# The product with w_down as seven block products, with weight sums made by adding transfers

## Chip, core, metric

The kernel runs on one core of one Trainium2 chip. The metric is device time in microseconds (us) of one launch. The engines are named as in the profile: PE (TensorE matrix products; PEld is its weight load), DVE (VectorE), ACT (ScalarE), POOL (GpSimd) and SP (SyncE, whose queue issues the transfers of this kernel). Each engine works through its own queue in order; an instruction whose semaphores have not come yet holds up all that stand behind it on that engine.

## What is computed

One decoder block on 1024 tokens of width 1024, in float32: a projection, sparse attention and stick-breaking attention, an output projection, and a gated MLP with a short convolution. The change concerns the last product of the MLP, `w_down`, of shape 2816 x 1024:

```python
u = _rms_norm(h, norm2_w[layer])
up = u @ w_up[layer]
up = lax.conv_general_dilated(up, conv_w[layer], ...) + conv_b[layer]   # causal, width 3
gate, val = up[..., :D_FF], up[..., D_FF:]                              # D_FF = 2816
h = h + (jax.nn.silu(gate) * val) @ w_down[layer]
return _rms_norm(h, final_norm_w)
```

## The kernel before

Each float32 operand is split into a high part of reduced precision (`hi`, made by ACT) and the rest (`lo = raw - hi`, made by DVE or POOL); a product is then three PE instructions, hi·hi, hi·lo and lo·hi, added up in PSUM. `split_w` (L191 to L194) makes the two parts: ACT on L193, the subtraction on L194, on POOL unless another engine is named.

The stages that matter here, in order of time:

- **Stick-breaking attention**, `sb_attend` (about 62 to 345 us). It runs over 48 units; a unit's front (`sb_front`) makes scores on PE (L425, L426, L428), two sigmoids on ACT (L429, L430), a scan on DVE (L436) and then, on POOL, the product `A = A * tt` (L439) and a clearing (L441). Two units later `sb_turn` lets PE transpose that `A` (L455). In between PE does, at a rate set by `PACE`, the projections of the next pair of heads (`sb_project`), whose weights come in halves of 256 KB by SP (L204) into tiles `wr`, and are split by ACT (L193) and POOL (L194) into `wh` and `wl`. These steps are generators; at each `yield` of the attention the caller may let another generator go one step further. The tile framework then fixes one order for each engine.
- **The product with w_up** (`up`, about 835 to 1239 us), already seven block products (P1 to P7) for each of 22 column blocks, with weight sums made on chip. Its result, gated, goes to DRAM as `act_d`, one tile of 128 x 1024 (128 of the 2816 rows, all tokens) for each block; DVE does most of the additions out of PSUM.
- **The product with w_down** (`down`, from 1239 us to the end). For each half `c` of the tokens (4 blocks of 128 rows) eight PSUM banks hold 4 row blocks x 2 column halves. Over the 22 blocks `i` of 128 rows of `w_down`, `load_w` brings a weight tile of 512 KB and splits it on ACT and POOL (`dh`, `dl`), `load_act` brings 256 KB of `act_d` and splits it on ACT and DVE (`ah`, `al`), and each block then has 8 x 3 PE instructions of 512 columns (L1588 to L1590). The first and last GROUP = 4 blocks run bank by bank, so that a bank's sum is ready early. Then the residual is added (L1624, DVE), the row sum of squares is taken (ACT), and the normalised row goes out (`finish`, L1570, L1571, L1574). The first four blocks are fetched during the last block of `up`.

The weights of `down` are read by SP as they are; nothing is done with them earlier in the program, and POOL issues no transfer anywhere.

Of the kernel before, what the change touches and what calls it, by code (L numbers as in the profile page):

```python
# [10 lines left out]
F32 = mybir.dt.float32  # L11
F32R = mybir.dt.float32r
# [68 lines left out]
class Kern:  # L81
# [479 lines left out]
                    nc.vector.memset(self.score[rows, i, cur + 1:16], NEG)  # L561


    def compress_in(self, kv, wp, vp):
# [503 lines left out]
    def run(self):  # L1068
# [15 lines left out]
        with self.pool("sbv", "right") as vp:  # L1084
            st_b, st_a = ExitStack(), ExitStack()
            stk = [None, st_b.enter_context(self.pool("stkb", "right"))]
            stk[0] = st_a.enter_context(self.pool("stka", "right"))
            ops = []
            with self.pool("xin") as xin:
                proj = self.sb_project(0, wp, stk[0], vp, ops, xin)  # L1090
                self.load_norm(xin, vp, mxs, proj, stk[1])
                for _ in proj:
                    pass
            with self.pool("sbw") as work:
                fill, due = iter(()), 0.0
                got = [ops, [], [], []]

                def start(p):
                    nonlocal fill
                    for _ in fill:  # L1100
                        pass
                    if p < 3:
                        fill = self.sb_project(p + 1, wp, stk[1 - p % 2], vp, got[p + 1])
                    else:
                        st_a.close()
                        fill = self.compress_keys(st_a.enter_context(self.pool("cin", "right")), wp, vp)
                    self.pace = PACE[p == 3]
# [7 lines left out]
                for _ in fill:  # L1115
                    pass
            st_a.close()
            st_b.close()
# [148 lines left out]
    def mlp(self, mxs):  # L1267
# [125 lines left out]
        for _ in fill:  # L1393
            pass
        st_r.close()
        self.weights, self.acts = {}, {}
        self.up(p1)
        self.down(st_up)

# [58 lines left out]
    def up(self, p1):  # L1458
# [3 lines left out]
        for i in range(NF):  # L1462
# [45 lines left out]
            u3 = self.scratch()  # L1508
            nc.vector.tensor_add(u3, bc, u2)
            if last:  # L1510
                for j in range(GROUP):
                    if j > 1:
                        self.load_w(j)
                    self.load_act(j, 0)
            bd = self.ps(tags[3])
            self.product(bd, i, "P5", True)

# [14 lines left out]
            gate(1)  # L1532


    def load_w(self, i):

        homes = ((self.qn, 0), (self.qn, 4), (self.mts, 4), (self.mts, 0))
        if i < 2 * len(homes):
            if i in self.weights:
                return  # L1540
            t, lo = homes[i // 2]
            v = t[:, lo:lo + 4].rearrange("p a b t -> p (a b t)")[:, 2048 * (i % 2):2048 * (i % 2) + 2048]
            dh, dl = v[:, 0:T], v[:, T:2048]
        else:
            dh, dl = (self.tl(self.dp, [P, T], t, 5, F32R) for t in ("dh", "dl"))
        raw = self.tl(self.rawp, [P, KT, P], "wr", 4).rearrange("p k c -> p (k c)")
        self.nc.sync.dma_start(raw, self.a["w_down"][i * P:(i + 1) * P, :])
        self.split_w(raw, dh, dl)
        self.weights[i] = (dh, dl)

    def load_act(self, i, c):

        if c == 0 and i < GROUP:
            raw = self.scratch()
            ah, al = (t[:, i, :] for t in self.R["P7"])
        else:
            raw = self.tl(self.dp, [P, 512], "ar", 3)
            ah, al = (self.tl(self.dp, [P, 512], t, 7, F32R) for t in ("ah", "al"))
        self.nc.sync.dma_start(raw, self.act_d[i][:, c * 512:c * 512 + 512])
        self.split_w(raw, ah, al, self.nc.vector)  # L1560
        self.acts[i, c] = (ah, al)

    def down(self, st_up):
        nc, a = self.nc, self.a
        weights, acts = self.weights, self.acts
        rows = []

        def finish(tb, y, ss):
            r = self.rstd(ss, 1, 1.0 / DM, True)
            nc.scalar.activation(y[:, 0:512], y[:, 0:512], AF.Copy, scale=r[:, 0:1])  # L1570
            nc.vector.scalar_tensor_tensor(y[:, 512:DM], hs[tb][:, 512:DM], r[:, 0:1], self.fnw[:, 512:DM],  # L1571
                                           op0=ALU.mult, op1=ALU.mult)
            for i in range(2):
                nc.sync.dma_start(a["out"][tb * P:(tb + 1) * P, i * 512:i * 512 + 512], y[:, i * 512:i * 512 + 512])  # L1574

        hs = {}
        with ExitStack() as st_2:
            for c in range(2):
                banks = {}

                def mms(i, tb, hf):
                    if (tb, hf) not in banks:
                        banks[tb, hf] = self.ps(("o", "z", "z", "z", "mb", "tr", "tr", "ma")[2 * tb + hf])
                    pd = banks[tb, hf]
                    ah, al = acts[i, c]
                    dh, dl = weights[i]
                    s, cs = slice(tb * P, tb * P + P), slice(hf * 512, hf * 512 + 512)
                    nc.tensor.matmul(pd, ah[:, s], dh[:, cs], start=i == 0, stop=False)  # L1588
                    nc.tensor.matmul(pd, ah[:, s], dl[:, cs], start=False, stop=False)  # L1589
                    nc.tensor.matmul(pd, al[:, s], dh[:, cs], start=False, stop=i == NF - 1)  # L1590

                def blocks(first, last, alone):

                    for i in range(first, last):
                        if (i, c) not in acts:
                            self.load_w(i)
                            self.load_act(i, c)
                        if not alone:
                            continue
                        for tb in range(4):  # L1600
                            for hf in range(2):
                                mms(i, tb, hf)

                blocks(0, GROUP, False)
                for tb in range(4):
                    for hf in range(2):
                        for i in range(GROUP):
                            mms(i, tb, hf)
                if c == 0:
                    st_up.close()  # L1610
                    self.dp = self.rawp = st_2.enter_context(self.pool("dp"))
                    self.fnw = self.tl(self.dp, [P, DM], "fnw")
                    nc.sync.dma_start(self.fnw, a["final_norm_w"].rearrange("(o c) -> o c", o=1).to_broadcast([P, DM]))
                blocks(GROUP, NF - GROUP, True)
                blocks(NF - GROUP, NF, False)
                for tb in range(4):
                    row = 4 * c + tb
                    h = hs[row] = self.tl(self.dp, [P, DM], "h", 4)
                    nc.sync.dma_start(h, self.h_d[row])
                    for hf in range(2):  # L1620
                        for i in range(NF - GROUP, NF):
                            mms(i, tb, hf)
                        cs = slice(hf * 512, hf * 512 + 512)
                        nc.vector.tensor_add(h[:, cs], banks[tb, hf], h[:, cs])  # L1624
                    y = self.tl(self.dp, [P, DM], "y", 3)
                    nc.gpsimd.tensor_mul(y[:, 0:512], h[:, 0:512], self.fnw[:, 0:512])
                    ss = self.square_sums(self.tl(self.nt, [P, 512], "na", 2), [h[:, 0:512], h[:, 512:DM]])
                    rows.append((row, y, ss))
                    if len(rows) > 1:
                        finish(*rows.pop(0))  # L1630
            while rows:
                finish(*rows.pop(0))


_INS = ["x", "norm1_w", "w_in", "cmp_pos_k", "cmp_pos_v", "cmp_k_w1", "cmp_k_w2", "cmp_v_w1", "cmp_v_w2",
# [27 lines left out]
```

## Time and profile before

| | us |
|---|---|
| median of 3 runs | 1492.44 |
| lowest and highest | 1489.34, 1494.07 |
| the profiled execution, device time | 1489.68 |
| its span, first to last instruction | 1487.9 |

| engine | busy us | share of the span |
|---|---|---|
| PE | 1432.7 | 96% |
| PEld | 1200.9 | 81% |
| DVE | 979.3 | 66% |
| ACT | 793.7 | 53% |
| POOL | 761.4 | 51% |

The profile is of one execution. Busy time does not count waiting, nor the issuing of transfers. PE's instructions overlap, so its rate is best read from the distance of two starts. A window's row gives, for a stretch of the span, each engine's busy time with the number of its instructions, the granted TensorE clock as a share of full speed, the mean busy share of the 16 DMA engines and the GB/s that they moved.

### The profile page before, as it was taken

The page shows a single profiled execution, that of the slowest core. Times are in us where ns is not written, and L with a number is a line of the kernel's source. Part 1 is how long each engine was busy: PE and PEld are TensorE (multiplying, and loading weights), DVE is VectorE, ACT ScalarE, POOL GpSimd, SP SyncE. Part 2 cuts the span into 40 slices and gives each one's busy share as a digit, 9 for nine tenths or more (in the row PEclk, how much of TensorE's full clock was granted, in tenths as well). Part 3 has the DMA queues.
Part 4 walks back from the last instruction along what each step waited for, and adds up shares of the span by engine and source line. Part 5 has one row for each costly group of instructions (what it writes and reads, how often), then busy time and mean ns, then how long its engine had stood idle before and what let it go on. Part 6 is the DMA issues. An engine that isn't in the chain of part 4 may idle for free. (4 is left out here: it accounts for less than half of the span.)

```text
span 1487.9 us, 21917 instructions
## 1 busy us (share of the span) xinstructions
PE 1432.7 (96%) x7619; PEld 1200.9 (81%) x7619; DVE 979.3 (66%) x2018; ACT 793.7 (53%) x1691; POOL 761.4 (51%) x727
## 2 busy tenths in 40 slices
PE   7999999999899999999998899999999999999998
PEld 5777777777788988998887778888888887888886
DVE  5587878775257899997438687777778775414112
ACT  6576676653368888887324444444444453324122
POOL 3355655562326667664132566666666664545043
PEclk9999999999999999999999999999999999999999
DMA  5200100325311010003340222222222233845321
GB/s 195 71 22 22 29 22 22 96 65 162 113 30 30 1 57 2 1 16 114 128 135 22 78 78 85 86 85 85 85 86 85 79 113 116 298 140 192 103 92 57
DMA packets 113354, 122.75 MB, mean 83 GB/s; under 512 B 6988, under 2 KB 84444, under 8 KB 112988
## 3 DMA queue, kind: packets, MB, share of 16 engines
q1 hardware_dynamic: 113244, 121.36, 25.4%
q8 instruction: 60, 0.98, 0.3%
q14 instruction: 50, 0.41, 0.1%
HBM read 96.58 MB, written 24.75 MB: 82 GB/s over the span
## 5 line engine op out<-in xcount | busy, mean ns | idle before, releaser
L194 POOL TENSOR_TENSOR gl<-mxs,gh 128x512 fp32r<-128x512 f32 x88 | 116.5, 1325 | 66.3 <-ACT gh L193 63.0
L439 POOL TENSOR_TENSOR A<-A,tt 128x384 f32<-128x384 f32 (+3 forms) x96 | 95.8, 1002 | 97.1 <-DVE tt L436 50.5
L194 POOL TENSOR_TENSOR gl<-wr,gh 128x512 fp32r<-128x512 f32 x66 | 85.7, 1301 | 103.2 <-ACT gh L193 80.5
L194 DVE TENSOR_TENSOR al<-ar,ah 128x512 fp32r<-128x512 f32 x40 | 42.1, 1063 | 128.6 <-ACT ah L193 110.4
L194 POOL TENSOR_TENSOR dl<-wr,dh 128x1024 fp32r<-128x1024 f32 x28 | 69.7, 2495 | 102.8 <-ACT dh L193 90.7
L186 DVE TENSOR_TENSOR pl<-ps_tr,ph 128x512 fp32r<-128x512 f32 (+1 forms) x175 | 111.9, 642 | 13.1 <-ACT ph L185 11.6
L185 ACT ACTIVATE ph<-ps_tr 128x512 fp32r<-128x512 f32 (+1 forms) x175 | 98.0, 563 | 42.0 <-PE ps_tr L455 24.8
L193 ACT ACTIVATE gh<-mxs 128x512 fp32r<-128x512 f32 x88 | 55.3, 629 | 65.3 <-PE ps_ma L1455 22.1
L436 DVE TENSOR_TENSOR_SCAN tt<-tt 128x384 f32<-128x384 f32 (+1 forms) x64 | 69.8, 1093 | 28.3 <-ACT tt L429 27.8
L194 POOL TENSOR_TENSOR wl<-wr,wh 128x512 fp32r<-128x512 f32 x40 | 54.9, 1377 | 62.2 <-ACT wh L193 60.4
L193 ACT ACTIVATE ah<-ar 128x512 fp32r<-128x512 f32 x40 | 25.0, 628 | 110.2 <-PE ps_ma L1589 101.5
L429 ACT ACTIVATE tt<-ps_z 128x384 f32<-128x384 f32 (+3 forms) x96 | 47.6, 496 | 43.0 <-PE ps_z L428 20.2
L734 POOL TENSOR_SCALAR lgw<-lgw,r,gates 128x640 f32<-128x640 f32 (+4 forms) x64 | 48.2, 764 | 36.4 <-DVE r L732 15.7
L193 ACT ACTIVATE gh<-wr 128x512 fp32r<-128x512 f32 x66 | 40.9, 623 | 43.3 <-DMA wr<-w_up_d 15.1
L219 PE MATMUL ps_ma<-uh,wh 128*128 128x512 f32 x136 | 60.4, 444 | 1.2 <-ACT wh L193 1.2
L220 PE MATMUL ps_ma<-ul,wh 128*128 128x512 f32 x136 | 55.2, 406 | 2.1 <-DVE ul L189 2.1
L221 PE MATMUL ps_ma<-uh,wl 128*128 128x512 f32 x136 | 55.2, 406 | 0.6 <-POOL wl L194 0.6
L455 PE MATMUL ps_tr<-ident,A 128*128 128x128 f32 x320 | 49.1, 277 | 6.4 <-DVE pl L186 2.6
L455 PEld LDWEIGHTS ps_tr<-ident,A 128*128 128x128 f32 x320 | 37.1, 142 | 16.0 <-DVE osb L501 3.2
L1483 ACT ACTIVATE na<-na 128x512 f32<-128x512 f32 x44 | 27.6, 628 | 39.9 <-DVE na L1479 39.9
L1434 DVE TENSOR_TENSOR mxs<-mxs,wr 128x512 f32<-128x512 f32 x22 | 35.3, 1604 | 19.8 <-POOL mxs L1433 19.7
L430 ACT ACTIVATE A<-ps_z 128x384 f32<-128x384 f32 (+3 forms) x96 | 47.4, 493 | 0.1
(683 smaller groups left out, 5193.5 us busy)
## 6 DMA issues: line engine op xcount, KB each, us to landing
wr<-w_up_d SPq DMA_DIRECT2D x44, 512.0 KB, 5.0
wr<-w_down_d SPq DMA_DIRECT2D x36, 512.0 KB, 4.7
act_d<-na SPq DMA_DIRECT2D x44, 256.0 KB, 3.9
wr<-w_in_d SPq DMA_DIRECT2D x40, 256.0 KB, 2.8
ar<-act_d SPq DMA_DIRECT2D x40, 256.0 KB, 2.5
h<-h_d SPq DMA_DIRECT2D x8, 512.0 KB, 4.7
out_d<-y SPq DMA_DIRECT2D x16, 256.0 KB, 2.2
mxs<-x_d SPq DMA_DIRECT2D x4, 512.0 KB, 3.5
```

The costliest lines, as they stand in the source:

```text
L185: nc.scalar.activation(hi, src, AF.Copy)
L186: nc.vector.tensor_sub(lo, src, f(hi))
L193: nc.scalar.activation(hi, raw, AF.Copy)
L194: (eng or nc.gpsimd).tensor_sub(lo, raw, f(hi))
L219: nc.tensor.matmul(out, lh, rh, start=(i == 0), stop=False)
L220: nc.tensor.matmul(out, lh, rl, start=False, stop=False)
L221: nc.tensor.matmul(out, ll, rh, start=False, stop=(i == last))
L429: nc.scalar.activation(tt[:, 0:w], z[:, :w], AF.Sigmoid, scale=-1.0)
L436: nc.vector.tensor_tensor_scan(rev, rev, rev, 1.0 if carry[j] is None else carry[j], op0=ALU.mult, op1=ALU.bypass)
L439: nc.gpsimd.tensor_mul(A[:, j, 0:w], A[:, j, 0:w], tt[:, 1:w + 1])
L455: nc.tensor.transpose(pt[:, kk * 256 + j * P:kk * 256 + (j + 1) * P], A[:, j, c0:c0 + P], self.ident)
L734: nc.gpsimd.tensor_scalar(lg[i][:, :L], lg[i][:, :L], r[:, i:i + 1], gate[:, i:i + 1], op0=ALU.mult, op1=ALU.mult)
```

## The change

**In `down`.** The 2816 rows of `w_down` are cut into two halves of 11 blocks, its columns into two halves of 512, and the tokens into two halves of 512. The product of these 2 x 2 blocks is made as seven products in the order P1, P6, P2, P7, P5, P4, P3, each of 11 steps ("units", 77 in all), 4 row blocks and 3 PE instructions of 512 columns. A unit `n` has an operand of activations and one of weights, both 128 x 512. `fetch` issues its transfers by SP, up to 7 units ahead; `halves` forms sums of activations where the product wants one (P6 two subtractions, P7, P5 and P3 one each, all on DVE), and splits both operands on ACT and DVE into one of eight places. Activations that are used again stay in SBUF (`a11`, `a22`, `s2`). PSUM holds four banks for a product; P2 goes on in P1's banks, P4 in P7's, P3 in P5's. `evacuate` adds the banks out, on DVE but for P1; `bring` adds sums to residuals on POOL. POOL no longer splits weights here.

**In `sb_attend`.** Four of the seven products (P5, P7, P6, P4) need sums of weight blocks. A new generator `down_sums` makes them in DRAM, in 4 x 11 tiles `td` of 128 x 512: 44 plain copies DRAM to DRAM issued by SP, and 44 transfers issued by POOL that add a block of `w_down` into the tile. For each of the 11 steps, P5 and P7 are copied from one block and added to once; P6 is copied from P5's sum and added to; P4 from P6's sum and added to. So each step is a chain of six transfers, and each waits for the one before. The generator goes one step at each `yield` of the attention.

```diff
+    def down_sums(self):
+        b = {(i, k): self.a["w_down"].rearrange("(i j p) (k c) -> i k j p c", i=2, p=P, k=2)[i, k] ...}
+        td = self.td = {t: [self.dram.tile([P, 512], F32, name=f"td{t}_{j}") for j in range(n)]
+                        for t in ("P5", "P7", "P6", "P4")}
+        for r in range(n + 5):
+            for lag, dst, src, add in ((0, "P5", b[0, 1], None), (0, "P7", b[0, 1], None), (1, "P5", None, b[0, 0]),
+                                       (1, "P7", None, b[1, 1]), (2, "P6", td["P5"], None), (3, "P6", None, b[1, 1]),
+                                       (4, "P4", td["P6"], None), (5, "P4", None, b[1, 0])):
+                j = r - lag
+                if not 0 <= j < n:
+                    continue
+                if add is None:
+                    nc.sync.dma_start(td[dst][j], src[j])
+                else:
+                    nc.gpsimd.dma_start(td[dst][j], add[j], accum_op=ALU.add)
+                for _ in range(2):
+                    yield
...
+                sums = self.down_sums()
                 for _ in self.sb_attend(start, work, mxs):
+                    next(sums, None)
                     due += self.pace
...
             if last:
                 for _ in range(AHEAD):
                     self.prepare()
-                self.load_w(0)
-                self.load_w(1)
+                for n in range(2):
+                    self.fetch(n)
+                    self.halves(n)
...
-    def load_w(self, i):
-    def load_act(self, i, c):
...
+    DOWN = ("P1", "P6", "P2", "P7", "P5", "P4", "P3")
+    def fetch(self, n):
...
+        if name == "P1":
+            v = act(0, 0, self.scratch() if n < GROUP else keep("a11"))
+        elif name == "P6":
+            v = act(0, 1, passing())
+            act(1, 1, keep("a22"))
+            if j < GROUP:
+                act(0, 0, keep("a11"))
+        elif name in ("P2", "P3"):
+            v = act(1, 0, passing())
+        w = self.scratch()
+        src = {"P1": rows(0)[:, 0:512], "P2": rows(1)[:, 0:512], "P3": rows(1)[:, 512:DM]}
+        nc.sync.dma_start(w, src[name] if name in src else self.td[name][j])
+    def halves(self, n):
...
+        if name == "P6":
+            s2 = kept["s2", j] = self.tl(self.dp, [P, 512], "s2", self.ND)
+            nc.vector.tensor_sub(s2, v, kept["a22", j])
+            nc.vector.tensor_sub(s2, s2, kept["a11", j])
+            v = s2
+        elif name == "P7":
+            v = self.tl(self.dp, [P, 512], "ar", 4)
+            nc.vector.scalar_tensor_tensor(v, kept["s2", j], -1.0, kept["a22", j], op0=ALU.mult, op1=ALU.subtract)
...
+        self.split_w(v, ah, al, nc.vector)
+        self.split_w(w, bh, bl, nc.vector)
...
+        def mms(n, tb):
+            ah, al, bh, bl = self.slots[n]
+            nc.tensor.matmul(bank, ah[:, s], bh, start=first and j == 0, stop=False, skip_group_check=not first)
+            nc.tensor.matmul(bank, ah[:, s], bl, start=False, stop=False, skip_group_check=not first)
+            nc.tensor.matmul(bank, al[:, s], bh, start=False, stop=j == ND - 1, skip_group_check=not first)
```

**The order on the engines.** PE, DVE and ACT have the same instructions in the same order as before up to the last block of `up`. POOL and SP do not.

On POOL, at the start of `sb_attend`. `wl114`, `wl117` and `wl175` are three splits of projection weights, `A101` is the first unit's `A`, and `td...` are the sums. Before:

```order
L194 TENSOR_TENSOR wl114_636<-wr112_634,wh113_635 128x512
L441 MEMSET A101_606 128x128
L194 TENSOR_TENSOR wl117_642<-wr115_640,wh116_641 128x512
L194 TENSOR_TENSOR wl175_919<-wr173_917,wh174_918 128x512
L441 MEMSET A118_646 128x128
L439 TENSOR_TENSOR A101_606<-A101_606,tt102_607 128x128
L439 TENSOR_TENSOR A101_606<-A101_606,tt104_618 128x256
```

After, the end of the same stretch (between `wl114` and these rows stand ten more adding transfers and the clearing of `A101`):

```order
L582 DMA tdP6_4_644<-w_down_d 128x512
L582 DMA tdP4_2_653<-w_down_d 128x512
L582 DMA tdP5_7_625<-w_down_d 128x512
L582 DMA tdP7_7_636<-w_down_d 128x512
L194 TENSOR_TENSOR wl117_687<-wr115_685,wh116_686 128x512
L582 DMA tdP6_5_645<-w_down_d 128x512
L582 DMA tdP4_3_654<-w_down_d 128x512
L582 DMA tdP5_8_626<-w_down_d 128x512
L194 TENSOR_TENSOR wl175_977<-wr173_975,wh174_976 128x512
L441 MEMSET A118_691 128x128
L439 TENSOR_TENSOR A101_606<-A101_606,tt102_607 128x128
L582 DMA tdP7_8_637<-w_down_d 128x512
```

Ten adding transfers stand ahead of `wl114` on POOL, seventeen (14 of them ahead of `wl117`) between it and the first product of `A101`, and the last seventeen between the products of the next five units, the 44th ahead of the product that before started at 89.38 us.

On SP, the same place. `wr115` to `wr234` are halves of projection weights, `bnear_d` and `bcmp_d` tables that go to DRAM. Before:

```order
L533 DMA bnear_d_461<-KA84_470 128x1024
L204 DMA wr115_640<-w_in_d 128x4x128
L536 DMA bcmp_d_462<-KB82_463 128x960
L204 DMA wr173_917<-w_in_d 128x4x128
L204 DMA wr176_923<-w_in_d 128x4x128
L204 DMA wr234_1186<-w_in_d 128x4x128
```

After, from `wr173` on:

```order
L204 DMA wr173_975<-w_in_d 128x4x128
L580 DMA tdP4_0_651<-tdP6_0_640 16x4096
L580 DMA tdP5_5_623<-w_down_d 128x512
L580 DMA tdP7_5_634<-w_down_d 128x512
L580 DMA tdP6_3_643<-tdP5_3_621 16x4096
L580 DMA tdP4_1_652<-tdP6_1_641 16x4096
L580 DMA tdP5_6_624<-w_down_d 128x512
L580 DMA tdP7_6_635<-w_down_d 128x512
L580 DMA tdP6_4_644<-tdP5_4_622 16x4096
```

Ten copies stand ahead of the second `bnear_d` on SP, 18 from there to `wr176`, and 16 behind; each copy out of a `td` tile waits for the adding transfer into it, and the loads of `wr` behind it wait with it.

On DVE, in the last block of `up`, whose additions are L1505, L1509 and L1518 (after: L1533, L1537 and L1545). Before:

```order
L1484 TENSOR_TENSOR na2901_13332<-na2901_13332,nb2888_13254 128x512
L1505 TENSOR_TENSOR mxs_89<-ps_tr2913_13380,mxs_89 128x512
L194 TENSOR_TENSOR P7l2306_9804<-mxs_89,P7h2305_9803 128x512
L1509 TENSOR_TENSOR mxs_89<-ps_tr2914_13394,mxs_89 128x512
L194 TENSOR_TENSOR P7l2306_9804<-mxs_89,P7h2305_9803 128x512 x3
L1518 TENSOR_TENSOR ps_tr2913_13380<-ps_ma2917_13428,mxs_89 128x512
```

After:

```order
L194 TENSOR_TENSOR qn_4037<-mxs_89,qn_4037 128x512 x2
L1511 TENSOR_TENSOR na2901_13464<-na2901_13464,nb2888_13386 128x512
L194 TENSOR_TENSOR qn_4037<-mxs_89,qn_4037 128x512
L1533 TENSOR_TENSOR mxs_89<-ps_tr2911_13516,mxs_89 128x512
L194 TENSOR_TENSOR qn_4037<-mxs_89,qn_4037 128x512
L1537 TENSOR_TENSOR mxs_89<-ps_tr2912_13530,mxs_89 128x512
L194 TENSOR_TENSOR qn_4037<-mxs_89,qn_4037 128x512 x2
L1545 TENSOR_TENSOR ps_tr2911_13516<-ps_ma2913_13556,mxs_89 128x512
```

Where four splits of activations stood among the last additions of `up`, the splits of activations and weights of the first units of `down` stand now, six of them here; more follow among the convolution's instructions.

## Rows read from the trace of the kernel before

**Rows 1.** The page: span, busy times by engine, and the queue's packets, MB, share.

```profile
span 1487.9 us, 21917 instructions
...
PE 1432.7 (96%) x7619; PEld 1200.9 (81%) x7619; DVE 979.3 (66%) x2018; ACT 793.7 (53%) x1691; POOL 761.4 (51%) x727
...
q1 hardware_dynamic: 113244, 121.36, 25.4%
```

**Rows 2.** Windows by stage: attention, `up`, `down` (columns in the first row).

```profile
core 0: us, PE busy (x) PEld busy (x) DVE busy (x) ACT busy (x) POOL busy (x), PEclk, DMA share, GB/s
62.00:345.00 283.00, 271.38 (x1591) 221.18 (x1590) 213.41 (x369) 184.22 (x393) 163.71 (x181) 0.99 0.15 39
835.00:1236.00 401.00, 398.44 (x1757) 328.64 (x1755) 318.32 (x447) 189.58 (x336) 250.59 (x185) 1.00 0.27 85
1239.00:1481.00 242.00, 239.84 (x1057) 197.99 (x1055) 68.99 (x84) 74.59 (x115) 95.42 (x54) 1.00 0.43 150
```

**Rows 3.** Timeline of PE: first and last product of `down` (start, duration).

```profile
1239.00 0.39 PE L1588 MATMUL ps_o<-qn,P7h 128*128 128x512 f32 x1
...
1480.33 0.39 PE L1590 MATMUL ps_ma<-dh,al 128*128 128x512 f32 x1
```

**Rows 4.** Waits of PE from 1215 us on (total, times, longest).

```profile
PE ps_o L1590 <- DVE al L194: 1.9, 1, 1.9
PE ps_ma L1454 <- DVE ps_tr L1518: 0.5, 1, 0.5
```

**Rows 5.** Groups by line from 1270 us (busy, mean ns), and line L194 on DVE (min/median/max).

```profile
L194 POOL TENSOR_TENSOR dl<-wr,dh 128x1024 fp32r<-128x1024 f32 x28 | 69.7, 2495 | 102.8 <-ACT dh L193 90.7 <-DMA h<-h_d 9.0 <-DMA wr<-w_down_d 3.0
L194 DVE TENSOR_TENSOR al<-ar,ah 128x512 fp32r<-128x512 f32 x36 | 35.6, 996 | 115.1 <-ACT ah L193 110.4 <-PE ps_o L1589 4.7
...
L193 ACT ACTIVATE ah<-ar 128x512 fp32r<-128x512 f32 x35 | 21.9, 629 | 106.3 <-PE ps_ma L1589 101.5 <-DMA ar<-act_d 3.2 <-DVE al L194 1.5
...
L194 DVE TENSOR_TENSOR al<-ar,ah x40: 675/694/2896, 1260.8 to 1443.1; 128x512 fp32r<-128x512 f32 x40
```

**Rows 6.** Timeline of POOL at the start of the attention.

```profile
47.55 1.28 POOL L194 TENSOR_TENSOR wl<-wr,wh 128x512 fp32r<-128x512 f32 x1
...
61.14 1.29 POOL L194 TENSOR_TENSOR wl<-wr,wh 128x512 fp32r<-128x512 f32 x1 [12.16 <-ACT wh L193]
...
66.47 1.37 POOL L439 TENSOR_TENSOR A<-A,tt 128x128 f32<-128x128 f32 x2 [1.17 <-DVE tt L432]
...
89.38 1.17 POOL L439 TENSOR_TENSOR A<-A,tt 128x512 f32<-128x512 f32 x1 [1.46 <-PE ps_tr L455]
```

**Rows 7.** Timeline of PE in the same place: transposes of `A` (L455).

```profile
67.96 0.60 PE L455 MATMUL ps_tr<-ident,A 128*128 128x128 f32 x4
...
72.57 0.55 PE L455 MATMUL ps_tr<-ident,A 128*128 128x128 f32 x3 [1.67 <-POOL A L439]
...
93.64 0.60 PE L455 MATMUL ps_tr<-ident,A 128*128 128x128 f32 x4
```

**Rows 8.** Windows around the start of the attention; columns as in rows 2.

```profile
20.00:45.00 25.00, 21.60 (x111) 15.23 (x109) 20.17 (x25) 14.19 (x24) 6.53 (x6) 1.00 0.34 109
45.00:62.00 17.00, 17.00 (x79) 13.90 (x79) 5.50 (x11) 6.16 (x11) 4.19 (x8) 1.00 0.21 62
62.00:80.00 18.00, 15.93 (x90) 12.05 (x88) 13.15 (x25) 13.51 (x31) 11.22 (x14) 1.00 0.13 30
80.00:100.00 20.00, 19.28 (x115) 15.96 (x115) 17.40 (x30) 14.55 (x31) 11.02 (x13) 1.00 0.10 26
100.00:130.00 30.00, 29.19 (x163) 23.24 (x163) 19.61 (x33) 17.93 (x39) 17.07 (x18) 1.00 0.10 26
```

**Rows 9.** Timeline of SP: issues of transfers (start, duration of issuing).

```profile
42.37 0.36 SPq L533 DMA_DIRECT2D bnear_d<-KA  x1
...
1247.88 0.37 SPq L1613 DMA_DIRECT2D fnw<-final_norm_w_d  x1
```

**Rows 10.** The page: issues of transfers, KB each, median us to landing.

```profile
ar<-act_d SPq DMA_DIRECT2D x40, 256.0 KB, 2.5
```

More of the change, by code (lines that the diff above doesn't have):

```diff
@@ L561, in load_tables @@
                     nc.vector.memset(self.score[rows, i, cur + 1:16], NEG)
+    def down_sums(self):
+        nc, n = self.nc, NF // 2
+        b = {(i, k): self.a["w_down"].rearrange("(i j p) (k c) -> i k j p c", i=2, p=P, k=2)[i, k]
+             for i in range(2) for k in range(2)}
+        td = self.td = {t: [self.dram.tile([P, 512], F32, name=f"td{t}_{j}") for j in range(n)]
[13 more added lines that the diff above has]
+                    yield
     def compress_in(self, kv, wp, vp):
@@ L1115, in run @@
                 for _ in fill:
+                    pass
+                for _ in sums:
                     pass
@@ L1395, in mlp @@
         st_r.close()
-        self.weights, self.acts = {}, {}
+        self.raw_ab, self.kept, self.slots = {}, {}, {}
         self.up(p1)
@@ L1510, in up @@
             if last:
[L1511 to L1514, printed above, removed]
+                for n in range(2, GROUP):
+                    self.fetch(n)
+                    self.halves(n)
             bd = self.ps(tags[3])
@@ L1532, in up @@
             gate(1)
-    def load_w(self, i):
[L1537 to L1549, printed above, removed]
@@ L1551, in load_act @@
-    def load_act(self, i, c):
[L1553 to L1561, printed above, removed]
-    def down(self, st_up):
[L1564 to L1576, printed above, removed]
-        with ExitStack() as st_2:
[L1578 to L1604, printed above, removed]
-                for tb in range(4):
[L1606 to L1632, printed above, removed]
@@ new lines, with act, keep, passing @@
+    ND = NF // 2
+    DOWN = ("P1", "P6", "P2", "P7", "P5", "P4", "P3")
+    def fetch(self, n):
+        nc = self.nc
+        name, j = self.DOWN[n // self.ND], n % self.ND
+        def act(b, c, t):
+            nc.sync.dma_start(t, self.act_d[j + b * self.ND][:, c * 512:c * 512 + 512])
+            return t
+        def keep(key):
+            t = self.kept[key, j] = self.tl(self.dp, [P, 512], key, self.ND)
+            return t
+        def passing():
+            return self.tl(self.dp, [P, 512], "ar", 4)
+        v = None
+        if name == "P1":
[8 more added lines that the diff above has]
+        w = self.scratch()
+        rows = lambda b: self.a["w_down"][(j + b * self.ND) * P:(j + b * self.ND + 1) * P, :]
+        src = {"P1": rows(0)[:, 0:512], "P2": rows(1)[:, 0:512], "P3": rows(1)[:, 512:DM]}
+        nc.sync.dma_start(w, src[name] if name in src else self.td[name][j])
+        self.raw_ab[n] = (v, w)
@@ new lines, in halves @@
+    def halves(self, n):
+        nc = self.nc
+        name, j = self.DOWN[n // self.ND], n % self.ND
+        v, w = self.raw_ab.pop(n)
+        kept = self.kept
+        if name == "P6":
[6 more added lines that the diff above has]
+            nc.vector.scalar_tensor_tensor(v, kept["s2", j], -1.0, kept["a22", j], op0=ALU.mult, op1=ALU.subtract)
+        elif name == "P5":
+            v = self.tl(self.dp, [P, 512], "ar", 4)
+            nc.vector.scalar_tensor_tensor(v, kept["s2", j], -1.0, kept["a11", j], op0=ALU.mult, op1=ALU.subtract)
+        elif name == "P4":
+            v = kept["a22", j]
+        elif name == "P3":
+            nc.vector.scalar_tensor_tensor(v, v, -1.0, kept["s2", j], op0=ALU.mult, op1=ALU.subtract)
+        t, lo = ((self.qn, 0), (self.qn, 4), (self.mts, 4), (self.mts, 0))[n % 8 // 2]
+        place = t[:, lo:lo + 4].rearrange("p a b t -> p (a b t)")[:, n % 2 * 2048:n % 2 * 2048 + 2048]
+        ah, al, bh, bl = (place[:, 512 * i:512 * i + 512] for i in range(4))
+        self.split_w(v, ah, al, nc.vector)
+        self.split_w(w, bh, bl, nc.vector)
+        self.slots[n] = (ah, al, bh, bl)
```

96 lines of the change are left out of this document (added).

## The prediction

> **What bounds the kernel now.** I read the busy times of the page first, then windows cut at the stages, then the timelines at the two places that the change touches. PE is busy for 96% of the span [rows 1], and 271.4 of 283 us of the attention, 398.4 of 401 of `up`, and 239.8 of 242 of `down` [rows 2]. Whatever takes instructions from PE shortens the time one for one, and whatever keeps PE waiting lengthens it the same way, because PE has almost nothing to make up with. The transfers are far from full: 0.15 of the DMA engines' time in the attention and 0.43 in `down` [rows 2]. So there are two questions: how much PE work goes from `down`, and whether the sums can be made at the start of the attention without making PE wait. All sums below are made on the profiled execution, 1489.68 us; the median of the three runs is 1492.44, so 2.8 us are added at the end. Differences under 0.3% (about 4.5 us) are about what a measurement of this kernel cannot tell from no change.
>
> **What `down` gains.** Before, PE issues 22 blocks x 8 banks x 3 = 528 instructions for each half of the tokens, 1056 in all. After, 77 units x 4 row blocks x 3 = 924 of the same 512 columns. First product at 1239.00, last at 1480.33 [rows 3], with one stall of 1.9 us on the way [rows 4]: (1480.33 - 1239.00 - 1.9) / 1055 = 0.227 us from start to start. 132 instructions less are 132 x 0.227 = 30.0 us less. The stall of 1.9 us is at the entry, where PE waits for the first splits on DVE; it goes with the code that made it, but the entry is now tighter. Its first group of four units holds 48 instructions (10.9 us) where four blocks held 96 (21.8 us), each needs a weight split on DVE too, and the first loads behind those issued in advance follow the place on SP where the final norm's weight is fetched, at 1247.88 [rows 9]; with 2.5 us to land [rows 10] and two splits, units 4 and up can be late. Between 0 (the loads issued ahead suffice) and 5 us (half of the 10.9) I take 3, nearest to the 1.9 seen at this place. More splits now stand among DVE's last additions of `up`. PE lost 0.5 us to DVE there [rows 4]; between 0 and eight more splits of 0.694 [rows 5], 6 us, I take 1. Together: -30.0 - 1.9 + 3 + 1 = **-27.9 us**, with bounds -32 and -21.
>
> **What could eat that inside `down`.** DVE: 154 splits (both operands of 77 units) and 55 sums (P6 22, P7, P5 and P3 11 each) are 209 operations. The split's median is 0.694 us, its mean from 1270 us on 0.996 [rows 5]. Apart from its 40 splits DVE had 69.0 - 40 x 0.996 = 29 us of work there [rows 2, 5], and has about as much after. At the median that is 209 x 0.694 + 29 = 174 us beside 924 x 0.227 = 210 us of PE; at the mean, 237 us, and DVE would be the bound. I take the median: it is the split's usual time, and what stretches some of them to 2.9 us has as its likeliest partner POOL's 28 splits of 2.5 us in the same window [rows 5], which the change removes. ACT: 154 splits x 0.629 = 97 us [rows 5] and, at most, the 53 us of its other work (74.6 - 35 x 0.629) are 150, under 210. Transfers: 136 operand tiles and 16 of the residual, 0.262 MB each, and 4.2 MB out are 44 MB in 210 us, 210 GB/s. The queue moved 121.36 MB in 25.4% of 1487.9 us [rows 1], that is 321 GB/s when all engines are busy, so a share of 0.65. Covered. The tail behind the last product (1480.7 to 1487.9) keeps its steps; nothing is booked for it.
>
> **What the sums cost.** Their places on the queues decide. Ten adding transfers stand on POOL ahead of the split at 47.55, seventeen between it and the first product of `A` at 66.47, and the other seventeen ahead of the product at 89.38 [rows 6]. On SP ten copies stand ahead of the issue at 42.37 [rows 9], 18 then follow before the last of three weight loads there, and 16 come later. Each is one link of a chain, copy, add, copy, add: POOL's queue stands until a copy has landed, SP's until an add has, and the work queued behind stands with them. On POOL that is the product `A`, and PE reads it at once: its first transposes start at 67.96, 1.5 us after, and the next waited 1.67 us for POOL [rows 7]. So a delay of that product is a delay of PE.
>
> How long do 44 copies and 44 adds take? Free time of the DMA engines, from their share in each window [rows 8]: 25 x 0.66 = 16.5 us from 20 to 45 us, 17 x 0.79 = 13.4 to 62, 18 x 0.87 = 15.7 to 80, 20 x 0.90 = 18.0 to 100, then 0.9 a microsecond. A 256 KB load costs 0.262 MB / 321 GB/s = 0.82 us of all engines. No row shows a transfer from DRAM to DRAM, nor one that adds. Lower bound: each moves as a load does, 0.82. Upper bound: each read and each write is paid for as a transfer of its own, 1.63 for a copy and 2.45 for an add. I take 0.82 for a copy, nearest to the load's row (one read, one write), and 1.63 for an add, as it reads two tiles where a load reads one.
>
> By 45 us: 10 x 0.82 + 10 x 1.63 = 24.5, less 16.5 free, leaves 8.0. Then 18 x 0.82 + 17 x 1.63 = 42.5, so 50.5 before the first `A`. 47.1 us are free by 100 us, and the last 3.4 take 3.8: done at 103.8 and not 66.5, +37.3 us. Then 16 x 0.82 + 17 x 1.63 = 40.8 us, 45.4 at 0.9, where 22.9 us (66.47 to 89.38) stood before: +22.4. Off go 3.1 us between the end of that product at 90.55 and its reader on PE at 93.64 [rows 6, 7], and PE's idle time from 62 to 100 us, 2.1 + 0.7 [rows 8]. The sums cost +37.3 + 22.4 - 5.9 = **+53.8 us**.
>
> The chain's delay alone does not set this: two of 2.5 us [rows 10] per two rounds, 16 rounds, are 40 us, under the 108 us of transfers. POOL's issuing has no row; between SP's 0.36 [rows 9] and a whole operation of POOL, 1.3 [rows 6], 17 of them are 6 to 22 us, inside the time in which it waits for transfers anyway.
>
> The Trainium skill speaks on this point. Its page "Collectives: The Full Stack", section "The bandwidth ceiling: the fold count and why AG ≠ RS ≠ AR", says that a reduction in the DMA path needs two source reads for each write and reaches about half of a copy's rate, 32.35 against 62.28 GB/s. No row here shows such a transfer; by that rule an add is two loads' time and the kernel comes out as I forecast, by the load's row alone it would be 1479 us.
>
> **Sum.** 1489.68 - 27.9 + 53.8 = 1515.6; with 2.8 for the median, **1518 us**.
>
> **Rivals.**
> *The adds run as loads do (faster).* The place is the same, POOL's queue ahead of the first `A`; the price of an add decides. At 0.82 all: 16.4 us by 45, nothing left over; 35 x 0.82 = 28.7 done at 79.5, +13.0; then 33 x 0.82 / 0.9 = 30.1 for 22.9, +7.2; less 5.9 is +14.3. 1489.7 - 27.9 + 14.3 + 2.8 = 1479. For it: the engines pass bytes, and an adder in their way need not cost time. Against: the second read. Between the two ends the cost grows by (53.8 - 14.3) / 0.81 = 48.8 us for each microsecond of an add; it equals the gain at 0.82 + (27.9 - 14.3) / 48.8 = 1.10 us. From there on the kernel is slower. An add between 1.0 and 1.2 us gives no change that can be measured.
>
> *Transfers inside DRAM are dear.* At 1.63 and 2.45: 40.8 - 16.5 = 24.3 left at 45 us; with 71.0 more, 95.3; 47.1 by 100 us and 53.6 after, 153.6, +87.1; then 67.7 / 0.9 = 75.3 for 22.9, +52.4; less 5.9, +133.6. 1598 us. For it: no row bounds the writing into DRAM beside the reading; against: the engines of a load read and write at the same time too.
>
> *`down` does not get what it is meant to.* DVE at 0.996 a time is the bound: 237 us, a gain of 5 and not 28; with the sums at 53.8 that is 1541 us. Against it stand the splits at 0.694 once POOL is away.
>
> **How the numbers follow.** Adds of about 1.2 to 2.3 us, 1498 to 1551 by 48.8 us for each: 0.38, the forecast. Adds as loads: 0.32, faster. An add near 1.1: 0.10, no change. Dear transfers, 1551 and up: 0.15. DVE the bound: 0.05, slower with either price of the adds. So faster 0.32, same 0.10, slower 0.58. The range reaches to the fast rival less the 9 us that the bounds of `down` and a POOL queue with more slack can add, 1470, and into the dear case up to 1580; about 0.06 is left out below and 0.08 above. The forecast's own range is 1498 to 1551.
>
> **What would show it.** After: in the attention's first 80 us, POOL idle ahead of the adds and ahead of the first product of `A`, released by transfers, and PE idle at its first transposes of `A`, some 35 us and then some 20 in pieces; the DMA share near 1 there; the attention later by about 54 us, the rest until `down` unchanged. In `down`, first to last product about 211 to 214 us, PE's waits under 5 us, DVE's splits at 0.69. The forecast is wrong if the share of the DMA engines stays low where POOL waits (then a delay, or the issuing, sets the pace and not the bytes), if PE waits for nothing there, or if `down` takes over 220 us.

## The result and the profile after

The kernel with the change takes 1513.34 us (median of 4 runs, 1512.12 to 1517.48) against 1490.89 us (4 runs). The ratio is 1.0153, with a 95% interval of 1.0125 to 1.018: slower, by 22 us. The profiled execution has a span of 1511.5 us against 1487.9 [rows 1], 23.6 us more.

Page of the changed kernel: span, busy times, DMA queues, the group of POOL's adding transfers, and its issues (KB each, us from issue to landing).

```profile
span 1511.5 us, 22302 instructions
...
PE 1414.0 (94%) x7487; PEld 1185.5 (78%) x7487; DVE 1075.1 (71%) x2191; ACT 821.3 (54%) x1769; POOL 722.4 (48%) x747
...
q1 hardware_dynamic: 126332, 138.14, 28.6%
q0 software_dynamic: 6336, 11.54, 4.7%
...
L582 POOL DMA_DIRECT2D tdP<-w_down_d x44 | 37.8, 891 | 60.9 <-issue 29.4
...
tdP<-w_down_d POOLq DMA_DIRECT2D x44, 256.0 KB, 7.0
```

PE is busy for 18.7 us less, and the span is longer by 23.6. A queue that was not there before, q0, moves the 11.54 MB of the 44 adds in 4.7% of 1511.5 us, which is 71 us of all engines: 1.61 us for each add.

Windows of the changed kernel at the start of the attention, to be held against [rows 8]; the last is `down`.

```profile
core 0: us, PE busy (x) PEld busy (x) DVE busy (x) ACT busy (x) POOL busy (x), PEclk, DMA share, GB/s
20.00:45.00 25.00, 21.62 (x100) 15.58 (x99) 17.91 (x22) 13.10 (x22) 11.84 (x12) 0.86 0.86 218
45.00:62.00 17.00, 17.00 (x81) 13.82 (x80) 8.01 (x12) 6.63 (x12) 9.69 (x13) 1.00 1.07 280
62.00:80.00 18.00, 8.56 (x44) 6.17 (x42) 3.19 (x9) 6.72 (x15) 4.93 (x6) 0.85 1.06 262
80.00:100.00 20.00, 0.48 (x1) 0.18 (x1) 0.84 (x3) 0.85 (x2) 9.63 (x12) 0.50 0.92 182
100.00:130.00 30.00, 22.75 (x110) 18.01 (x110) 17.14 (x27) 14.54 (x30) 18.00 (x23) 0.84 1.01 219
...
1292.80:1502.40 209.60, 209.60 (x925) 173.30 (x923) 163.41 (x248) 100.79 (x189) 34.33 (x31) 1.00 0.56 189
```

From 45 to 130 us the DMA engines are full where before they were busy for 0.10 to 0.21. PE has one instruction from 80 to 100 us. In `down` PE is busy without a gap.

POOL at the same place: the last issues ahead of the first product of `A`, and the 44th add with the product that stood at 89.38 us before [rows 6].

```profile
66.59 0.81 POOL L582 DMA_DIRECT2D tdP<-w_down_d  x1 [5.11 <-DMA tdP<-tdP]
...
96.49 0.83 POOL L582 DMA_DIRECT2D tdP<-w_down_d  x1 [1.34 <-issue]
97.03 1.58 POOL L194 TENSOR_TENSOR wl<-wr,wh 128x512 fp32r<-128x512 f32 x1
...
98.40 0.71 POOL L439 TENSOR_TENSOR A<-A,tt 128x128 f32<-128x128 f32 x1
...
141.51 0.82 POOL L582 DMA_DIRECT2D tdP<-w_down_d  x1 [1.55 <-DVE tt L432]
142.07 1.37 POOL L439 TENSOR_TENSOR A<-A,tt 128x512 f32<-128x512 f32 x1
```

In all, POOL stands for 60.9 us ahead of the adds. The three largest parts of that by what ended them (us, times):

```profile
  issue: 29.4, 20
  DMA tdP<-w_down_d: 13.6, 5
  DMA tdP<-tdP: 7.9, 3
```

So 21.5 us are waits for transfers, as forecast. "issue" is idle time for which the profile names nothing that POOL waited for; what POOL stands for in these 29.4 us is not shown.

What PE waits for from 60 to 400 us (total, times, longest), and the product at which the longest wait ends:

```profile
PE ps_tr L455 <- POOL A L439: 37.1, 4, 28.2
PE ps_tr L455 <- DVE pl L186: 10.9, 8, 6.8
```

```profile
99.17 0.48 PE L455 MATMUL ps_tr<-ident,A 128*128 128x128 f32 x1 [28.23 <-POOL A L439]
```

Forecast were some 35 us in one piece and then some 20 in several.

And PE at both ends of `down`, which answers to [rows 3]:

```profile
1292.81 0.39 PE L1651 MATMUL ps_o<-qn 128*128 128x512 f32 x1
...
1502.02 0.39 PE L1653 MATMUL ps_z<-mts 128*128 128x512 f32 x1
```

So the whole difference lies in three places. `down` starts 53.8 us later (1292.81 against 1239.00), takes 209.2 us from first to last product where it took 241.3, and the tail behind the last product (start of it plus 0.39) is 9.1 us where it was 7.2: 53.8 - 32.1 + 1.9 = 23.6. The last transpose of `A` starts at 393.2 us against 340.4, so 52.8 of the 53.8 us are there at the attention's end.

### The profile page after: what moved, and what is told of

The parts are those of the page before. It is cut to its first block, busy times and chain, and to the rows that moved or that the text cites. A ratio compares the mean times of both kernels' runs of the same rounds, so it can differ in the third digit from the quotient of the medians.

```text
span 1511.5 us, 22302 instructions
## 1 busy us (share of the span) xinstructions
PE 1414.0 (94%) x7487; PEld 1185.5 (78%) x7487; DVE 1075.1 (71%) x2191; ACT 821.3 (54%) x1769; POOL 722.4 (48%) x747
## 3 DMA queue, kind: packets, MB, share of 16 engines
q0 software_dynamic: 6336, 11.54, 4.7%
## 5 line engine op out<-in xcount | busy, mean ns | idle before, releaser
L194 POOL TENSOR_TENSOR gl<-mxs,gh 128x512 fp32r<-128x512 f32 x88 | 116.4, 1323 | 71.8 <-ACT gh L193 68.5
L194 POOL TENSOR_TENSOR gl<-wr,gh 128x512 fp32r<-128x512 f32 x66 | 85.7, 1300 | 103.4 <-ACT gh L193 78.6
L455 PE MATMUL ps_tr<-ident,A 128*128 128x128 f32 x320 | 50.7, 281 | 50.5 <-POOL A L439 37.1
L436 DVE TENSOR_TENSOR_SCAN tt<-tt 128x384 f32<-128x384 f32 (+1 forms) x64 | 69.6, 1089 | 30.3 <-ACT tt L429 28.7
L455 PEld LDWEIGHTS ps_tr<-ident,A 128*128 128x128 f32 x320 | 37.2, 143 | 61.8 <-POOL A L439 47.5
L1687 POOL TENSOR_TENSOR a<-a,p 128x512 f32<-128x512 f32 x8 | 12.5, 1571 | 141.0 <-DVE mts L194 121.5
L194 POOL TENSOR_TENSOR wl<-wr,wh 128x512 fp32r<-128x512 f32 x40 | 56.0, 1404 | 29.1 <-ACT wh L193 27.0
L582 POOL DMA_DIRECT2D tdP<-w_down_d x44 | 37.8, 891 | 60.9 <-issue 29.4
L219 PE MATMUL ps_ma<-uh,wh 128*128 128x512 f32 x136 | 63.6, 468 | 1.4 <-ACT wh L193 1.4
L436 DVE TENSOR_TENSOR_SCAN tt<-tt,tt 128x256 f32<-128x256 f32 (+1 forms) x32 | 41.7, 1303 | 23.7 <-issue 12.0
L219 PE MATMUL ps_mb<-late,wh 128*128 128x512 f32 x112 | 47.1, 421 | 0.0
```

The lines of the kernel that those rows point to most:

```text
L194: (eng or nc.gpsimd).tensor_sub(lo, raw, f(hi))
L219: nc.tensor.matmul(out, lh, rh, start=(i == 0), stop=False)
L436: nc.vector.tensor_tensor_scan(rev, rev, rev, 1.0 if carry[j] is None else carry[j], op0=ALU.mult, op1=ALU.bypass)
L455: nc.tensor.transpose(pt[:, kk * 256 + j * P:kk * 256 + (j + 1) * P], A[:, j, c0:c0 + P], self.ident)
```

## The experiments

My theory was that of the prediction: a gain in `down` and a loss at the start of the attention that simply add up, the loss because POOL's queue stands while the DMA engines work off 44 adds that cost them twice a load's time. The rivals for the loss: POOL's issuing (the count), and the waits from link to link of the chain. The measure of the loss is the last transpose of `A` (L455), at 340.4 us before.

**The product without its sums.**

```diff
-                sums = self.down_sums()
+                sums = iter(())
-        nc.sync.dma_start(w, src[name] if name in src else self.td[name][j])
+        nc.sync.dma_start(w, src[name])        # P5, P7, P6, P4: one block of w_down
```

> The new product alone: no sums are made, and P5, P7, P6 and P4 take one block of w_down where they would take a sum, so the result of that product is not the reference's. My theory (the change is a gain in the product with w_down and a loss at the start of the attention that simply add up): the attention ends as before, at 345 us, `down` takes 210 us from first to last product and the tail about 2 us more than before: 1490.9 - 31 + 2 = 1462 us. Rival (the product gains less, and something else in the new kernel gave the rest back or took it): 1470 us or more.

Measured 1459.45 us (1458.53 to 1460.45) against 1491.91, ratio 0.9782 (0.9760 to 0.9804). The last transpose starts at 340.3 us. The product by itself is worth 32 us.

**The sums without the product.** `down_sums` and its calls are put into the kernel before, and nothing reads the sums.

```diff
+                sums = self.down_sums()
                 for _ in self.sb_attend(start, work, mxs):
+                    next(sums, None)
```

> The kernel before, with the 44 copies and 44 adds at the same place and no reader for them. My theory: the whole loss of the attention and none of the gain, 1490.9 + 52.8 = 1544 us, the attention's first transposes at about 99 us. Rival (the loss comes in part from the way the new product is read and ordered): below 1530 us.

Measured 1546.33 us in one run, 54.4 above the kernel before; the last transpose at 395.2 us. Gain and loss add up: 1491.9 - 32.5 + 54.4 = 1513.8, and the change takes 1513.3.

**Plain transfers in place of the adds.**

```diff
-                    nc.gpsimd.dma_start(td[dst][j], add[j], accum_op=ALU.add)
+                    nc.gpsimd.dma_start(td[dst][j], add[j])
```

> The 44 transfers of POOL copy a block and no longer add, so four products get wrong weights; issuer, count, places and bytes named by the instructions are as in the change. Bytes theory (an adding transfer holds the DMA engines for 1.6 us where a plain one holds them for 0.8, and that is what POOL waits for): the sums cost 14 us and not 53, so about 1513 - 38 = 1475 us, the first product of A at about 80 us. Count theory (POOL's issuing of 44 transfers sets the pace): 1513 us as it is. Chain theory (each link waits for the one before to land): 1490 to 1505 us, as only the landing gets shorter.

Measured 1486.74 us in one run; the last transpose at 366.6 us, a loss of 26.2 us and not 52.8. Queues of this kernel and then of the changed one, both from 20 to 150 us (packets, MB, share):

```profile
q0 software_dynamic: 3520, 11.54, 28.1%
```

```profile
q0 software_dynamic: 6336, 11.54, 54.7%
```

28.1% of 130 us over 44 is 0.83 us, as a load [rows 1]; 54.7% is 1.62 us. The price of adding is shown. But an add also moves in 144 packets (6336 / 44) and a plain transfer in 80, and POOL's idle time by "issue" falls from 29.4 to 2.0 us with it; so half of the loss goes with the adding and the packets together, and this run does not part them. The other half is more than the 14 us that I expected of plain transfers; the rest of the runs deal with it.

**The chain cut.**

```diff
-  (2, "P6", td["P5"], None), (4, "P4", td["P6"], None)
+  (2, "P6", b[0, 0], None), (4, "P4", b[0, 0], None)
```

> The copies for P6 and P4 read w_down and not the sums of P5 and P6, so the chain of six links is cut into two-link ones and P6 and P4 get wrong weights; bytes, counts and issuers stay. Bytes theory: 1513 us, within 6. Count theory: 1513 us. Chain theory: 20 us or more faster, 1490 us or less.

Measured 1515.53 us in one run, the last transpose at 397.3 us. Cutting the chain of six into pairs gains nothing; that rival is out.

**Why an add costs twice: half the pieces.**

```diff
-  nc.gpsimd.dma_start(td[dst][j], add[j], accum_op=ALU.add)
+  nc.gpsimd.dma_start(td[dst][j].rearrange("(a b) c -> a (b c)", b=2),
+                      self.a["w_down"][64 * j:64 * j + 64, :], accum_op=ALU.add, max_dma_last_dim=4096)
```

> Each add takes 64 rows of 4 KB where it took 128 rows of 2 KB: the same 256 KB in half the pieces (the sums are then wrong, and the adds stand a little more spread on POOL). It tells why an add holds the engines twice as long as a plain transfer: if it is the bytes (two read for one written), the queue of POOL's transfers holds its 1.6 us for each; if it is the pieces (144 packets against 80 in the plain one), it falls to about 0.9 us, and the time to about 1490 us.

Its queue of adds from 20 to 150 us:

```profile
q0 software_dynamic: 3520, 11.54, 50.9%
```

With as many packets as the plain transfers had, an add still takes 50.9% x 130 / 44 = 1.50 us. So it is not the pieces. Whether it is the second read or the adding itself isn't shown: the records count the bytes of an add once. The time, 1475.60 us, says nothing on the price, since the adds stand more spread on POOL in this kernel: 19 and not 27 of them ahead of the first product of `A`, which runs at 75.20 us.

The pieces do go with something else. POOL's idle time by "issue" ahead of the adds is 0.5 us here and 2.0 with the plain transfers, both of 80 packets, and 29.4 in the change and 29.8 with the chain cut, both of 144. No run has 144 packets and adds nothing, so how much of the loss comes from their number stays open.

**An eighth of the bytes.**

```diff
-  nc.gpsimd.dma_start(td[dst][j], add[j], accum_op=ALU.add)
+  nc.gpsimd.dma_start(td[dst][j][:16], add[j][:16], accum_op=ALU.add)
```

> Each add takes 16 of its 128 rows, an eighth of the bytes (three products get wrong weights in the other rows); count, places, copies and the chain stay. Bytes theory: copies 44 x 0.7 and adds 44 x 0.2 us are 40 us of the DMA engines, so nothing is left over at 45 us and the loss is under 10 us: about 1463 to 1470 us. If what is left of the loss with plain transfers (27 us, not 14) is the chain and the issuing, some 15 us stay: 1475 us or more.

Measured 1471.40 us in one run, between the two; the last transpose at 354.2 us, a loss of 13.8 us with an eighth of the added bytes (q0 takes 9.1% from 20 to 150 us, 0.27 us an add). So the bytes theory was not the whole of it. POOL's first product of `A` and the twelfth, the one that stood at 89.38 us before:

```profile
72.34 2.25 POOL L439 TENSOR_TENSOR A<-A,tt 128x128 f32<-128x128 f32 x1
...
101.81 1.08 POOL L439 TENSOR_TENSOR A<-A,tt 128x512 f32<-128x512 f32 x1 [0.73 <-PE ps_o L475]
```

Between them POOL waits 0.6 us for a transfer and 2.2 us for other engines, and is at work for the rest; yet they lie 29.5 us apart where it was 22.9. So POOL's own work sets the pace there, with 17 issues among its products, and makes 6.6 us of the loss. The 5.9 us by which the first one is late can still be the copies, whose bytes are unchanged.

**The sums spread over the attention.** Each add is queued behind a product of `A`, each copy behind a weight load, some two links a unit.

```diff
+            self.behind["POOL"] = ...      # the product A * tt of this unit
...
+                    with self.tc.issue_after(self.behind["POOL"]):
                         nc.gpsimd.dma_start(td[dst][j], add[j], accum_op=ALU.add)
```

> The same 88 transfers, but each queued behind a later instruction: the adds on POOL behind a product of A of their own unit, the copies on SP behind a weight load, so that about one add and one copy come to each of the 48 units of the attention (5.8 us a unit; 1.62 + 0.7 us of the DMA engines), and a link's predecessor stands some four units earlier. My theory (the loss is only that POOL stands waiting for bytes that pile up in one place): the engines have 0.85 of 283 us free, POOL does not wait for transfers, and the loss falls from 53 us to 0 to 12 us (44 issues of 0.82 us on POOL, some of them late for A): 1460 to 1472 us, clearly faster than before. Rival (POOL's issuing or the adds slow the attention wherever they stand): 1480 us or more.

Measured 1475.95 us (1473.33 to 1477.71) against 1493.37, ratio 0.9876 (0.9858 to 0.9894): faster than the kernel before, and 16 us above the product without sums. The loss falls from 52.8 to 14.7 us (last transpose at 355.1) and not to 0 to 12; the time lies between what my theory and its rival gave. POOL waits for no transfer ahead of an add here.

**The same with an eighth of the bytes**, by the edit of the run with small adds.

> The spread sums of e5_spread with adds of 16 rows of 128 (wrong weights in the other rows): POOL's 44 issues stay, an eighth of the added bytes. If what is left of the loss there (16 us) is POOL's issuing and what it does to the instructions beside it on POOL and DVE: still 1470 us or more. If it is the bytes (transfers of the attention that come later for them): below 1465 us.

Measured 1469.98 us in one run, last transpose at 350.8 us. 10.4 of the 14.7 us stay with an eighth of the added bytes. Of these, 1.9 are there at the first product of `A` (68.35 against 66.47), which no add stands ahead of. The rest comes with POOL's issuing and what it does beside it, but also with the 44 copies, which are unchanged; a run with the copies alone was not made, so their share is not shown. DVE's scans (L436, here L440), of the product without sums and then of the spread sums, from 62 to 400 us (min/median/max):

```profile
L436 DVE TENSOR_TENSOR_SCAN tt<-tt x64: 425/960/1905, 66.1 to 326.6; 128x384 f32<-128x384 f32 x24, 128x512 f32<-128x512 f32 x24, 128x128 f32<-128x128 f32 x8, 128x256 f32<-128x256 f32 x8
L436 DVE TENSOR_TENSOR_SCAN tt<-tt,tt x32: 742/1284/1845, 74.0 to 331.2; 128x256 f32<-128x256 f32 x16, 128x512 f32<-128x512 f32 x16
```

```profile
L440 DVE TENSOR_TENSOR_SCAN tt<-tt x64: 424/1136/2803, 67.4 to 340.0; 128x384 f32<-128x384 f32 x24, 128x512 f32<-128x512 f32 x24, 128x128 f32<-128x128 f32 x8, 128x256 f32<-128x256 f32 x8
L440 DVE TENSOR_TENSOR_SCAN tt<-tt,tt x32: 741/1354/3593, 75.2 to 346.0; 128x256 f32<-128x256 f32 x16, 128x512 f32<-128x512 f32 x16
```

**The sums in another stage**, `up`: with each weight split from the second column block on one link, an add behind that split on POOL or a copy behind the last weight load on SP.

```diff
-                sums = self.down_sums()          # in the attention
+        self.drops = self.down_sums()            # ahead of up
...
         self.split_w(v, hi, lo)
+        self.behind["POOL"] = ...
+        for _ in range(self.items):
+            next(self.drops, None)
```

> The same sums, moved to the product with w_up: from its second block on, one link behind each weight split of POOL (an add) or behind a weight load of SP (a copy), some seven links in a block of 18 us; they end by about block 14 of 22. There PE's operands are prepared several products ahead, POOL is busy for 62% and DVE for 79%. My theory (an add costs POOL 0.84 us, stretches what DVE and POOL do beside it, and 1.6 us of the DMA engines; all of it is free where PE does not read POOL's and DVE's result at once): the attention as before, the sums cost 0 to 3 us, 1460 to 1464 us. Rival (the adds cost wherever they stand): 1470 us or more, with PE waiting in `up`.

Measured 1464.71 us (1463.33 to 1466.69) against 1492.58, ratio 0.9820 (0.9795 to 0.9845). This version makes the same sums and is faster than both kernels. Its windows in the attention, in `up` and in two stretches of `up` in which adds are issued:

```profile
62.00:345.00 283.00, 270.56 (x1593) 220.17 (x1592) 214.68 (x369) 184.42 (x393) 161.69 (x181) 1.00 0.14 39
...
835.00:1236.00 401.00, 397.65 (x1752) 328.34 (x1751) 319.30 (x449) 188.54 (x336) 270.98 (x225) 1.00 0.54 136
...
900.00:1000.00 100.00, 100.00 (x443) 82.85 (x442) 79.75 (x111) 47.35 (x86) 74.03 (x65) 1.00 0.73 178
1000.00:1100.00 100.00, 100.00 (x443) 82.85 (x442) 79.66 (x115) 48.12 (x86) 75.03 (x66) 1.00 0.74 168
```

The same adds, no cheaper (POOL busy for 74 of 100 us, DMA engines for 0.73), leave PE without a gap where it does not read POOL's result at once. The time is just over the 1464 us of my theory. Of the 5 us to the product without sums 4.4 lie at the start of `up`, and nothing is lost after it. The product without sums and then this kernel, from 820 to 890 us:

```profile
820.00:890.00 70.00, 64.57 (x297) 52.06 (x297) 53.24 (x79) 31.53 (x56) 39.69 (x29) 0.98 0.27 83
```

```profile
820.00:890.00 70.00, 62.80 (x278) 50.54 (x278) 54.00 (x77) 30.56 (x54) 39.80 (x32) 0.93 0.53 147
```

PE does 278 instructions instead of 297, at a lower granted clock. Some 1.7 of the 4.4 us are there before the first add, which is issued at 856.78, with copies already on their way; what part the copies, the first adds and the clock have in this is not parted.

## Why the prediction was right, point by point

**The gain in `down`: right, and a little larger.** Forecast -27.9, measured -32.1 from first to last product. The 132 instructions x 0.227 = 30.0 and the 1.9 us stall are there; the 4 us that I took off for a tight entry and for DVE's additions were not needed, as PE names no wait from 1215 us on. The tail, for which nothing was booked, is 1.9 us longer.

**DVE as the bound: did not come.** Two groups of the splits of `down` in the changed kernel (min/median/max), which answer to [rows 5]:

```profile
L194 DVE TENSOR_TENSOR qn<-mxs,qn x36: 678/685/1780, 1305.1 to 1482.8; 128x512 fp32r<-128x512 f32 x36
L194 DVE TENSOR_TENSOR mts<-ar,mts x22: 678/692/883, 1338.0 to 1487.4; 128x512 fp32r<-128x512 f32 x22
```

DVE is busy for 163 of 209.6 us; the forecast was 174.

**The loss of the sums: right in its place and in its main cause; that its sum came within 1 us, +52.8 at the last transpose against 53.8 forecast, is luck, as terms that were off cancelled.** Right were the price of an add, 1.62 us against 1.63, that of a copy (in the windows from 20 to 350 us of the spread sums and of the product alone, q1 takes 27.3% and 16.1% of 330 us: 37 us for 44 copies, 0.84 each, against 0.82), the full DMA engines, and PE's wait for POOL's `A` (37.1 us). Here the rule of the Trainium skill that I had weighed (page "Collectives: The Full Stack", section "The bandwidth ceiling: the fold count and why AG ≠ RS ≠ AR", half of a copy's rate, stated for collectives) agrees with the trace in its ratio, 1.62 to 0.83; its reason, two reads, no run here shows.

The forecast's own terms, beside what the traces show (us; the twelfth product of `A` is the one at 89.38 us before, and at 142.07 in the changed kernel):

| | adds, forecast | adds, measured | plain, forecast | plain, measured |
|---|---|---|---|---|
| first product of `A` later by | 37.3 | 31.9 | 13.0 | 16.2 |
| from there to the twelfth, longer by | 22.4 | 20.8 | 7.2 | 10.2 |
| from there to the last transpose | -5.9 | +0.1 | -5.9 | -0.2 |
| loss | 53.8 | 52.8 | 14.3 | 26.2 |

The two products with plain transfers:

```profile
82.71 0.41 POOL L439 TENSOR_TENSOR A<-A,tt 128x128 f32<-128x128 f32 x1
...
115.81 1.10 POOL L439 TENSOR_TENSOR A<-A,tt 128x512 f32<-128x512 f32 x1
```

- *Too much: the wait for the last adds.* I let the first `A` wait until the 27th add is done, at 103.8 us. POOL goes on once an add is issued: the last one ahead of that product is issued at 96.49 and, with the median of 7.0 us, lands at about 103.5; the product runs at 98.40. From plain to adding transfers the loss grows by (52.8 - 26.2) / (1.62 - 0.83) = 34 us for each microsecond of an add, where I had 48.8.
- *Too much: what I took off.* Nothing of the 5.9 us was absorbed, with adds or without. The 3.1 us between the twelfth product and its reader on PE are no reserve: it ends at 143.44, and PE reads it at 146.27, after a wait for DVE:

```profile
146.27 1.09 PE L455 MATMUL ps_tr<-ident,A 128*128 128x128 f32 x4 [6.77 <-DVE pl L186]
```

- *Too little: the issuing.* I had put POOL's issuing inside its waiting, at no price. Each add's issue holds POOL for a median of 0.82 us, and in the run with small adds that makes 6.6 us between the two products. With plain transfers both delays are 3 us longer than the bytes gave; whether that is the issuing too, no run shows.
- *Not booked: the clock.* Before, PE did 440 instructions in 76.4 us of work from 62 to 142 us (0.174 each); after, 184 in 38.28 (0.208). The granted clock falls to 0.50 (1.2 of 2.4 GHz) while PE stands for 28.2 us. 184 x 0.034 = 6 us is an estimate, as the two stretches do not hold the same instructions; that it is what kept PE from making up the 5.9 us is not shown. The windows from 62 to 142 us, of the kernel before and of the changed one:

```profile
62.00:142.00 80.00, 76.40 (x440) 61.39 (x439) 59.24 (x105) 54.17 (x116) 43.31 (x50) 1.00 0.11 27
```

```profile
62.00:142.00 80.00, 38.28 (x184) 29.46 (x182) 23.17 (x43) 23.86 (x51) 39.23 (x49) 0.74 0.99 214
```

**The fast rival** had the right lever, the price of an add, but too low a floor: with transfers at a load's price the kernel takes 1487 us in one run, not 1479, and 5 us less than the kernel before, hardly more than the 4.5 us that the forecast took as no change.

## What to carry to other kernels

Price work that is "moved into the transfers" three times: by the bytes at the engines' full share (an adding transfer at twice a plain one here), by the issue on the engine that must issue it, and by what stands behind that issue in its queue. The last decided: the same 88 transfers cost 53 us ahead of a product that PE reads at once, 15 us spread between such products, and about 5 us in a stage where operands are made several products ahead. Here the first sum is fetched at 1285 us, more than 1100 us after the last add was issued. When a result has that much time, look for the stage with slack, and pin the transfers behind an instruction of it: left alone, the order that was made here has 27 of the 44 adds ahead of the first product of `A`.

## What was new of the hardware

- By the queue's share, an add of 256 KB in DRAM holds the DMA engines for 1.62 us, a plain transfer by the same queue for 0.83, and with 80 packets instead of 144 the add still takes 1.50. With the adds spread over the attention it is not less (24.8% of 330 us, 1.86 us).
- In these kernels issuing costs POOL more for an add than for a plain transfer of the same shape. The 44 issues of the changed kernel and of the one with plain transfers (ns, min/median/max):

```profile
L582 POOL DMA_DIRECT2D tdP<-w_down_d x44: 777/826/1426, 25.8 to 141.5; - x44
```

```profile
L582 POOL DMA_DIRECT2D tdP<-w_down_d x44: 523/523/988, 24.7 to 115.3; - x44
```

- DVE's scans last longer among the spread sums (rows above). One scan of 128x384, which has a mean of 1.04 us in the product without sums, took 2.80 us beside two issues and the split behind them:

```profile
174.09 2.80 DVE L440 TENSOR_TENSOR_SCAN tt<-tt 128x384 f32<-128x384 f32 x1 [1.14 <-ACT tt L433]
```

```profile
173.08 1.67 POOL L589 DMA_DIRECT2D tdP<-w_down_d  x2
174.44 1.63 POOL L195 TENSOR_TENSOR wl<-wr,wh 128x512 fp32r<-128x512 f32 x1
```

The Trainium skill, page "SBUF — State Buffer", section "SBUF: two separate sides", says that an operation of DVE with two inputs in SBUF and one of GpSimd that reads SBUF exclude each other on a pair of ports: whichever starts first holds the pair to its end. The rows do not decide whether that is at work: the split begins 0.35 us after the scan and ends 0.82 us before it, and no run parts the issues from the split.
